# Six staging places at the turn into the down stages, a first tile's norm in eight pieces, and ones-products behind a tile's first chunk

## The chip, the core and the metric

One Trainium2 core runs the whole program. Its engines are TensorE (PE, matmuls, with a separate weight load, PEld), VectorE (DVE), ScalarE (ACT), GpSimd (POOL) and SyncE (SP), which only issues transfers here. Each engine works through its own instructions in order, and semaphores tie them together. The metric is the device time of one execution in microseconds; the median of the runs is compared.

## The reference

The reference is one step of a streaming encoder on 1072 columns (16 meta tokens, 1024 prompt frames, 32 sample frames), with 1024 features:

```python
def rmsnorm(x, g):
    return x * rsqrt(mean(x * x) + EPS) * g

def half_ffn(x, g, w_gate, w_up, w_down):
    h = rmsnorm(x, g)
    return x + 0.5 * ((silu(h @ w_gate) * (h @ w_up)) @ w_down)

x = half_ffn(x, ffn1_norm, ...)
h = rmsnorm(x, mix_norm)
qa, ka, va, zf, ih, qh, g, ga, gb = split(h @ w_in)
oa = stick_breaking_attention(qa, ka, va)      # with the cache for the sample
ob, S = hgrn(qh, sigmoid(zf), ih)              # chunked linear recurrence
x = x + (sigmoid(ga) * (oa @ w_a) + sigmoid(gb) * (norm(ob) * silu(g) @ w_b)) @ w_out
x = half_ffn(x, ffn2_norm, ...)
y = rmsnorm(x, final_norm)
```

The hidden width of both half_ffn is 2816. Outputs are y, the new keys and values, and the final recurrent states.

## The kernel before

**Products.** Every float32 operand is split into a high half (ACT copies it to a rounded type, line 219) and a low half (DVE subtracts, line 220), and each product is made of three matmuls: high by high, high by low, low by high. Line 202 and line 203 do the same for plain weights.

**The two feed-forward blocks** (`Seven`) use seven products of half-size blocks where eight are due. The seven operands made of an activation block are named B11, T3, B21, T2, T4, T1 and B22. The hidden features come in eleven units of 256. The up stage works through the units one after the other, the gate half and then the up half, seven product groups in each (`unit`, `rest`). When a unit is done, `send` queues seven stagings for it. A staging makes one operand (for a T a subtraction on DVE, line 343), splits it into a staging place on chip and lets POOL start the write to `mid_dram` (line 353). `tick`, called after each product group, lets one staging of the unit before go at every odd group. Normal units alternate between two places, called R and st. The last unit's seven stagings, made at the turn into the down stage, take their places from a list (line 325); a place taken a second time must wait until its first write has landed.

**The down stage** (`down`) reads these operands back: `load` and `load_rest` fetch a unit's seven operands into its homes, among them the small tiles xe0, xe1, xe2, xe3 and st in the first block, and mh and st in the second. Its weights come through `lanes` (raw loads, line 528, and sums into S, lines 542 to 545). Its first four jobs use one unit and half of the columns (`singles`), with 84 matmuls; the first and the last stagings are sent around them (`sends(4)`, `sends(3)`). Then come jobs with two units at once, and six singles at the end. A job has seven products p1 to p7: after p1 ACT copies the sum to a second bank (line 600), and the results go out on ACT (line 594) or are added by DVE (line 591). Activation columns are 268 wide per quarter in the first block and 264 in the second.

**Behind the first down stage** comes the next norm, in three column tiles of 400, 384 and 288. `normalise` makes the scaled high and low halves (xh on ACT, xl on DVE, lines 234 and 235), squares them on ACT and adds the squares up, five on POOL into `ms` and three on DVE into `ys` (lines 240 to 244). `finish` multiplies both sums by a matrix of ones on PE and makes R, the scale of the columns, from it. `after1(0)` does the first tile in one go while the last three jobs of down run, and the first `finish` is called after `down`. `project_all` then makes the zf projection: for each tile, three chunks, one for each of three weights, 24 matmuls each, with the rest of the `finish` calls between them.

**What sets the order.** A tile framework gives each engine its list. Instructions are placed by the order of the program and by a priority; PE, while `PE.on` is set, keeps exactly the order in which the code issues (`InOrder`). The buffers of a tag rotate, and a reuse waits until the last reader of the buffer is done.

## Time and profile before

| | us |
|---|---|
| median of three runs | 2502.78 |
| lowest and highest | 2499.66, 2502.88 |
| profiled execution | 2499.49 |
| its span, first to last instruction | 2497.4 |
| PE busy in it | 2403.0 (96%) |
| DVE busy | 1669.2 (67%) |
| ACT busy | 1021.3 (41%) |
| mean granted PE clock | 0.990 |

The profiled execution lies 2.1 us above its own span and 3.3 us under the median. PE is the engine that is busy nearly throughout, and the up stages run without a gap on it. A stretch in which PE stands still or runs at a lower clock is therefore where time can be won or lost. An idle engine that is not PE costs nothing by itself. In a timeline row the bracket at the end gives the idle time of the engine before the instruction and what ended it. A windows row gives the stretch, its length, then busy time and count of PE, PEld, DVE, ACT and POOL, the granted PE clock as a share, the busy share of the transfer engines and GB/s.

### The profile page before, as it was taken

What the parts mean: (1) busy time and instruction counts of PE and PEld (TensorE: products, weight loads), DVE (VectorE), ACT (ScalarE), POOL (GpSimd) and SP (SyncE); (2) the same over time, 40 slices, a digit from 0 to 9 for tenths busy, and PEclk for the clock granted to TensorE, in tenths of its full rate; (3) what the DMA queues carried; (4) which work ended last, traced back from release to release, by engine and by line L of the source; (5) the groups of instructions that cost most, each with busy time, mean ns of one, the idle gap of its engine ahead of it and who ended that gap; (6) DMA issues with size and microseconds to landing.
All of it is one profiled execution on the core that took longest, in us unless ns stands there. A gap on an engine that the chain in (4) does not pass through costs nothing.

```text
span 2497.4 us, 47900 instructions
## 1 busy us (share of the span) xinstructions
PE 2403.0 (96%) x19500; PEld 2299.1 (92%) x19500; DVE 1669.2 (67%) x3144; ACT 1021.3 (41%) x2129; POOL 257.2 (10%) x461
## 2 busy tenths in 40 slices
PE   6999999989998999999999999999799999989997
PEld 5999999979998999999788888999799999989997
DVE  4767676758865377774666665556966767666876
ACT  6444444542225243332545544323544444443223
POOL 1001010100003011221000000111011111110000
PEclk9999999999999999999999999999899999999999
DMA  7334343477651211111211122522244444467761
GB/s 197 105 122 166 122 166 122 164 292 280 245 210 62 60 44 56 48 49 53 57 44 49 44 64 67 190 86 98 75 136 153 143 147 147 143 266 267 274 235 71
DMA packets 270371, 331.93 MB, mean 133 GB/s; under 512 B 41078, under 2 KB 228726, under 8 KB 264518
## 3 DMA queue, kind: packets, MB, share of 16 engines
q1 hardware_dynamic: 247942, 244.96, 29.7%
q0 software_dynamic: 22208, 83.91, 8.9%
q8 instruction: 153, 2.51, 0.4%
q14 instruction: 68, 0.56, 0.1%
HBM read 213.93 MB, written 114.89 MB: 132 GB/s over the span
## 4 chain that ended last, share of the span: by engine, by line
PE 54%; issue 29%; DVE 6%; DMA 4%; POOL 4%; ACT 3%; POOLq 0%; SPq 0%; DVEq 0%; ACTq 0%
PE ps_mm L103 20%; PE ps_z L103 11%; PE pu L103 6%; PE ps_o L103 5%; PE pv L103 4%; PE pf L103 4%; POOL mid_dram L353 3%; DMA mid_dram<-st 2%; PE ps_tr L103 2%; PE ps_tr L106 2%; PE ps_z L106 1%; DMA u_xl<-mid_dram 1%; DVE wlo L203 1%; PE ps_mm L106 0%; DVE acc L1661 0%
## 5 line engine op out<-in xcount | busy, mean ns | idle before, releaser
L103 PE MATMUL ps_mm<-xh,whi 128*128 128x384 f32 (+2 forms) x952 | 316.8, 333 | 0.5 <-DVE raw L1455 0.5
L103 PE MATMUL ps_mm<-xh,wlo 128*128 128x384 f32 (+2 forms) x952 | 310.4, 326 | 0.0
L103 PE MATMUL ps_mm<-xl,whi 128*128 128x384 f32 (+2 forms) x952 | 309.9, 326 | 0.0
L219 ACT ACTIVATE whi<-S 128x1024 fp32r<-128x1024 f32 x122 | 129.2, 1059 | 310.7 <-PE ps_z L103 138.0
L353 POOL DMA_DIRECT2D mid_dram<-st x148 | 102.7, 702 | 872.7 <-DVE st L220 854.9
L103 PEld LDWEIGHTS ps_mm<-xh,whi 128*128 128x128 f32 x952 | 179.3, 188 | 9.0 <-issue 5.0
L103 PEld LDWEIGHTS ps_mm<-xl,whi 128*128 128x128 f32 x952 | 179.4, 188 | 1.1
L103 PEld LDWEIGHTS ps_mm<-xh,wlo 128*128 128x128 f32 x952 | 179.5, 189 | 0.3
L220 DVE TENSOR_TENSOR wlo<-S,whi 128x1024 fp32r<-128x1024 f32 x122 | 149.2, 1223 | 37.8 <-ACT whi L219 35.2
L220 DVE TENSOR_TENSOR st<-g,st 128x536 fp32r<-128x536 f32 (+1 forms) x148 | 103.5, 709 | 100.2 <-ACT st L219 100.1
L1247 DVE TENSOR_TENSOR_SCAN left<-left,oneb 128x512 f32<-128x512 f32 (+6 forms) x112 | 107.4, 959 | 54.8 <-ACT left L119 54.2
L202 ACT ACTIVATE whi<-raw 128x1024 fp32r<-128x1024 f32 x67 | 70.5, 1056 | 172.6 <-PE ps_mm L103 135.8
L219 ACT ACTIVATE st<-g 128x536 fp32r<-128x536 f32 (+1 forms) x148 | 93.5, 643 | 96.6 <-DMA mid_dram<-st 82.4
L220 DVE TENSOR_TENSOR wlo<-raw,whi 128x1024 fp32r<-128x1024 f32 x80 | 76.6, 958 | 72.6 <-ACT whi L219 70.9
L103 PE MATMUL ps_z<-acc1s,whi 128*128 128x268 f32 (+1 forms) x480 | 106.3, 285 | 0.0
L103 PE MATMUL ps_z<-xh1s,whi 128*128 128x268 f32 (+1 forms) x360 | 102.8, 286 | 0.0
L103 PE MATMUL ps_z<-xl1s,whi 128*128 128x268 f32 (+1 forms) x360 | 102.6, 285 | 0.0
L103 PE MATMUL ps_z<-xh1s,wlo 128*128 128x268 f32 (+1 forms) x360 | 102.6, 285 | 0.0
L103 PE MATMUL ps_z<-xh2s,whi 128*128 128x268 f32 (+1 forms) x352 | 100.5, 286 | 2.2 <-ACT s L458 2.2
L103 PE MATMUL ps_z<-xl2s,whi 128*128 128x268 f32 (+1 forms) x352 | 100.4, 285 | 0.0
L103 PE MATMUL ps_z<-xh2s,wlo 128*128 128x268 f32 (+1 forms) x352 | 100.3, 285 | 0.0
L203 DVE TENSOR_TENSOR wlo<-raw,whi 128x1024 fp32r<-128x1024 f32 x67 | 82.8, 1240 | 23.3 <-ACT whi L202 23.1
(719 smaller groups left out, 7636.2 us busy)
## 6 DMA issues: line engine op xcount, KB each, us to landing
mid_dram<-st POOLq DMA_DIRECT2D x74, 536.0 KB, 4.2
mid_dram<-st POOLq DMA_DIRECT2D x74, 528.0 KB, 3.9
raw<-in_ffn_w_gate_dram SPq DMA_DIRECT2D x44, 512.0 KB, 3.8
raw<-in_ffn_w_up_dram SPq DMA_DIRECT2D x44, 512.0 KB, 3.9
raw<-in_w_in_dram SPq DMA_DIRECT2D x44, 512.0 KB, 3.7
raw<-in_ffn_w_down_dram SPq DMA_DIRECT2D x40, 512.0 KB, 5.3
u_xl<-mid_dram SPq DMA_DIRECT2D x8, 1608.0 KB, 6.5
u_xh<-mid_dram SPq DMA_DIRECT2D x8, 1608.0 KB, 10.4
```

Of the source, the lines that this page charges most:

```text
L103: return self.queue(nc.tensor.matmul(*args, **more))
L106: return self.queue(nc.tensor.transpose(*args, **more))
L202: A.activation(hi, raw, AF.Copy)
L203: V.tensor_tensor(lo, raw, hi.bitcast(F32), op=ALU.subtract)
L219: A.activation(dst_h, src, AF.Copy)
L220: V.tensor_tensor(dst_l, src, dst_h.bitcast(F32), op=ALU.subtract)
L353: nc.gpsimd.dma_start(self.mids[i, :, :, NAMES.index(name)], st.bitcast(F32))
L1247: V.tensor_tensor_scan(rev(st[:rows]), rev(st[:rows]), one, 1.0 if carry is None else carry[:rows], op0=ALU.mult, op1=ALU.mult)
```

## The change

It has five parts. The last unit's stagings take six places in place of four, two of them new: the early tiles `e`, which are the first two of the three homes of unit 2 (xe0 and xe1 in the first block, two of mh in the second). Stagings of the other units go out at even instead of odd product groups, and in the gate half of the last unit at every group. The last single job at the turn and the last of the pair jobs are marked "end", which swaps the order of their last products. The norm of the first 400 columns becomes eight works, one for each feature block, that are taken from the queue at every second product of the last jobs (20 // 8 = 2); its POOL sum is kept in R. The tiles of 384 and 288 columns first make all their scaled halves and then all their squares, with DVE's sum in a tile of its own. Last, each `finish` is called behind a tile's first zf chunk.

```diff
@@ -227,29 +227,45 @@
         tag, bufs = homes.get(tag, (tag, bufs))
         return pool.tile([P, width[0]], F32, tag=tag, name=f"t_{tag}", bufs=bufs)
 
-    def normalise(pool, srcs, xh, xl, j, R, t0, n):
+    def normalise(pool, srcs, xh, xl, j, R, t0, n, together=True):
+
         s = slice(t0, t0 + n)
-        for k in range(KC):
+        tots = {}
+
+        def gain(k):
             g = gains[:, j, k:k + 1]
-            A.activation(xh[:, k, s], srcs[k], AF.Copy, scale=g)
+            made = A.activation(xh[:, k, s], srcs[k], AF.Copy, scale=g)
+            if together:
+                tc.add_manual_dep(made.ins, mark[0].name, order, reason="order")
             V.scalar_tensor_tensor(xl[:, k, s], srcs[k], g, xh[:, k, s].bitcast(F32),
                                    op0=ALU.mult, op1=ALU.subtract)
-        tots = []
-        for first, last, eng in ((0, 5, G), (5, KC, V)):
-            tot = temp(pool, "ys" if tots else "ms", 1)
-            A.activation(tot[:, :n], srcs[first], AF.Square)
-            for k in range(first + 1, last):
+
+        def square(k):
+            first = k < 5
+            if first not in tots:
+                tots[first] = R[:, s] if first else (
+                    temp(pool, "ys", 1) if together else
+                    pool.tile([P, width[0]], F32, tag="g", name="tot", bufs=4))[:, :n]
+                A.activation(tots[first], srcs[k], AF.Square)
+            else:
                 sq = temp(pool, "sq")
                 A.activation(sq[:, :n], srcs[k], AF.Square)
-                eng.tensor_tensor(tot[:, :n], tot[:, :n], sq[:, :n], op=ALU.add)
-            tots.append(tot)
+                (G if first else V).tensor_tensor(tots[first], tots[first], sq[:, :n], op=ALU.add)
+            if len(tots) == 2 and k == 7:
+                waiting.append(finish)
 
         def finish():
             ps = bank(rotate=True)
-            PE.matmul(ps[:, :n], ones, tots[0][:, :n], start=True, stop=False)
-            PE.matmul(ps[:, :n], ones, tots[1][:, :n], start=False, stop=True)
+            PE.matmul(ps[:, :n], ones, tots[True], start=True, stop=False)
+            PE.matmul(ps[:, :n], ones, tots[False], start=False, stop=True)
             scale_rows(pool, ps, R, t0, n)
-        waiting.append(finish)
+
+        def both(k):
+            gain(k)
+            square(k)
+        if together:
+            return [lambda k=k: both(k) for k in (0, 5, 1, 2, 6, 3, 4, 7)]
+        return [lambda k=k: gain(k) for k in range(KC)] + [lambda k=k: square(k) for k in (0, 5, 1, 2, 6, 3, 4, 7)]
 
     waiting = []
 
@@ -322,7 +338,7 @@
             self.mids, self.homes = mids, homes
             self.B, self.X, self.ahead = {}, {}, {}
             self.gs, self.later, self.groups = [], [], 0
-            self.stages = ["R", "st", "s", "s", "R", "st", "s"]
+            self.stages = ["R", "e", "e", "st", "s", "s", "R"]
 
         def tile(self, name, shape, dt=F32):
             tag, bufs = self.tags[name]
@@ -347,6 +363,8 @@
                         st = base.tile(shape, F32R, tag="R", name="st")
                     elif at == "st":
                         st = self.pool.tile(shape, F32R, tag="st", name="st", bufs=1)
+                    elif at == "e":
+                        st = self.early.pop(0)
                     else:
                         st = self.tile(at, shape, F32R)
                     split(st[:, :, 0], st[:, :, 1], v)
@@ -361,9 +379,9 @@
             away("T2", b22, b22, b11)
             away("T4", b21, b21, b22)
 
-        def tick(self):
+        def tick(self, every=2):
             self.groups += 1
-            if self.later and self.groups % 2:
+            if self.later and self.groups % every == 0:
                 self.later.pop(0)()
 
         def block(self, w, c):
@@ -478,7 +496,7 @@
                 for step in steps:
                     for b in range(2):
                         step(b)
-                    self.tick()
+                    self.tick(1 if i == FC // 2 - 1 else 2)
 
         def rest(self):
             for i in range(1, FC // 2):
@@ -626,12 +644,12 @@
 
             def run(jobs):
 
-                queue, count = [], [0]
+                queue, count, every = [], [0], [1]
 
                 def step(product):
                     product()
                     count[0] += 1
-                    if queue and count[0] % 5 == 0:
+                    if queue and count[0] % every[0] == 0:
                         queue.pop(0)()
                 before = None
                 for job in jobs:
@@ -644,6 +662,7 @@
                         step(before.p7)
                         if before.done:
                             queue += before.done()
+                            every[0] = max(1, 20 // len(queue))
                     step(job.p3 if job.done == "end" else job.p4)
                     if job.done == "end":
                         step(job.p6)
@@ -669,6 +688,8 @@
             PE.on = True
             W = self.lanes(w, ((0, 2), (0, 3)))
             units.update({i: self.Home(self, i) for i in range(2)})
+            self.early = [self.pool.tile([P, 2, 2, qw], F32R, tag=tag, name="st", bufs=bufs)
+                          for tag, bufs in self.homes[2][:2]]
             for i in range(2):
                 units[i].load_rest()
                 units[i].load(0)
@@ -676,7 +697,9 @@
             for i in range(2):
                 units[i].load(1)
             ahead = self.lanes(w, ((0, 0), (1, 0)), ("raw2", None))
-            run([Job([(units[0], W, l)], 2 + l, b) for b in range(2) for l in range(2)])
+            jobs = [Job([(units[0], W, l)], 2 + l, b) for b in range(2) for l in range(2)]
+            jobs[-1].done = "end"
+            run(jobs)
             sends(3)
             adds = {2: (0,), 3: (4,), 4: (1, 2), 5: (5, 6), 6: (3,), 7: (7,)}
 
@@ -691,7 +714,10 @@
                         if mp % 2:
                             for m in adds.get(s, ()):
                                 add_residual(m)
-                        yield Job([(units[s - 1], W, 0), (units[s], W, 1)], mp)
+                        job = Job([(units[s - 1], W, 0), (units[s], W, 1)], mp)
+                        if s == last and mp == 2:
+                            job.done = "end"
+                        yield job
 
             psum("pairs")
             run(steps())
@@ -871,14 +897,18 @@
             if "R" not in fed:
                 fed.update(xh=big("xh", F32R), xl=big("xl", F32R), R=base.tile([P, T], F32, tag="R", name="R"))
             flat = [a.rearrange("p q n -> p (q n)") for a in ff.acc]
-            for t0, n in TT[1:] if b else TT[:1]:
+            works = []
+
+            def keep(t0, n):
                 for m in range(KC):
                     nc.sync.dma_start(x1_dram[:, m, t0:t0 + n], flat[m][:, t0:t0 + n])
-                normalise(pool, [a[:, t0:t0 + n] for a in flat], fed["xh"], fed["xl"], 1, fed["R"], t0, n)
-            return []
+            for t0, n in TT[1:] if b else TT[:1]:
+                keep(t0, n)
+                works += normalise(pool, [a[:, t0:t0 + n] for a in flat], fed["xh"], fed["xl"], 1, fed["R"], t0, n,
+                                   not b)
+            return works
 
         ff.down(ffn1_w_down, x0_dram, "natural_log_exp_and_others", after1, early1)
-        waiting.pop(0)()
         xh1, xl1, R1 = fed["xh"], fed["xl"], fed["R"]
         homes.clear()
 
@@ -898,11 +928,11 @@
                                      for k in range(KC)])
                     if pending:
                         pending.pop()()
+                    if between and wh is ws[0][0]:
+                        between()
                     later = evac(ps, t0, n)
                     if later:
                         pending.append(later)
-                    if between:
-                        between()
             if pending:
                 pending.pop()()
 
@@ -922,7 +952,7 @@
             return COL_ZF + h * P, evac
 
         PE.on = True
-        project_all([zf_unit(h) for h in range(3)], TT, True, lambda: waiting and waiting.pop(0)(),
+        project_all([zf_unit(h) for h in range(3)], TT, True, lambda: waiting.pop(0)(),
                     [fed["w"]])
         PE.on, PE.last = False, None
```

How the instructions stand on the engines, of before and of the change, at three places:

ACT at the first turn, before. `whi<-S` is the split of weights, `st<-g` and `s<-g` are staging splits of hidden features, `ps_z<-ps_z` is the copy of a job's first sum, `acc1s` are evictions.

```order
L219 ACTIVATE whi<-S 128x1024
L219 ACTIVATE st<-g 128x2x268
L600 ACTIVATE ps_z<-ps_z 128x268
L594 ACTIVATE acc1s<-ps_o 128x268
L594 ACTIVATE acc1s<-ps_z 128x268
L219 ACTIVATE s<-g 128x2x268
L219 ACTIVATE st<-g 128x2x268
L594 ACTIVATE acc1s<-ps_z 128x268
```

The same place of the change (line 600 is now 618, 594 is 612):

```order
L219 ACTIVATE whi<-S 128x1024
L219 ACTIVATE s<-g 128x2x268
L618 ACTIVATE ps_z<-ps_z 128x268
L612 ACTIVATE acc1s<-ps_o 128x268
L612 ACTIVATE acc1s<-ps_z 128x268
L219 ACTIVATE st<-g 128x2x268 x2
L612 ACTIVATE acc1s<-ps_z 128x268
```

The staging split ahead of the first copy is another one, which goes into a tile that no earlier staging has used.

DVE at the end of the first down stage, before. `xl_8300` and `xl_8301` are the low halves of the tiles of 384 and 288 columns, `wlo<-raw,whi` is the low half of a zf weight; the second zf weight's is the first of the two here.

```order
L591 SCALAR_TENSOR_TENSOR acc0s<-ps_o,acc0s 128x268
L203 TENSOR_TENSOR wlo<-raw,whi 128x1024
L591 SCALAR_TENSOR_TENSOR acc0s<-ps_z,acc0s 128x268
...
L235 SCALAR_TENSOR_TENSOR xl_8300<-acc2s,gains,xh_8297 128x384 x2
L235 SCALAR_TENSOR_TENSOR xl_8301<-acc2s,gains,xh_8298 128x288
L235 SCALAR_TENSOR_TENSOR xl_8301<-acc0s,gains,xh_8298 128x288
L244 TENSOR_TENSOR t_ys<-t_ys,t_S 128x384
L235 SCALAR_TENSOR_TENSOR xl_8301<-acc1s,gains,xh_8298 128x288
L244 TENSOR_TENSOR t_ys<-t_ys,t_S 128x384
L203 TENSOR_TENSOR wlo<-raw,whi 128x1024
```

The same place of the change, from the last eviction of the down stage on (line 609):

```order
L609 SCALAR_TENSOR_TENSOR acc0s<-ps_z,acc0s 128x268
L240 SCALAR_TENSOR_TENSOR xl_8300<-acc0s,gains,xh_8297 128x384 x2
L240 SCALAR_TENSOR_TENSOR xl_8300<-acc1s,gains,xh_8297 128x384 x3
L240 SCALAR_TENSOR_TENSOR xl_8300<-acc2s,gains,xh_8297 128x384 x2
L253 TENSOR_TENSOR tot<-tot,t_S 128x384
L240 SCALAR_TENSOR_TENSOR xl_8301<-acc0s,gains,xh_8298 128x288
L240 SCALAR_TENSOR_TENSOR xl_8301<-acc1s,gains,xh_8298 128x288 x2
L240 SCALAR_TENSOR_TENSOR xl_8301<-acc2s,gains,xh_8298 128x288
L253 TENSOR_TENSOR tot<-tot,t_S 128x384
L240 SCALAR_TENSOR_TENSOR xl_8301<-acc2s,gains,xh_8298 128x288
L203 TENSOR_TENSOR wlo<-raw,whi 128x1024
```

The low half of the second zf weight has moved from among the evictions to behind the low halves of both later tiles.

PE in the last jobs of the first down stage, before (`cst` holds the ones):

```order
L103 MATMUL ps_z<-u_xl_7791,raw_8093 128x268
L103 MATMUL ps_tr<-t_ms,cst 128x400
L103 MATMUL ps_z<-u_xh_7559,whi 128x268 x2
...
L103 MATMUL ps_z<-u_xl_7791,raw_8093 128x268
L103 MATMUL ps_tr<-t_ys,cst 128x400
L103 MATMUL ps_z<-u_xe_7561,whi 128x268 x2
```

And the change, where they now stand:

```order
L103 MATMUL ps_tr<-xl_8299,whi 128x400
L103 MATMUL ps_tr<-xh_8296,wlo 128x400
L103 MATMUL ps_z<-R,cst 128x400
L103 MATMUL ps_z<-t_ys,cst 128x400
L103 MATMUL ps_o<-xh_8296,whi 128x400
```

The two ones-products of the first tile have left the products of the down stage and stand between the first zf chunk and the second.

## Rows read from the trace of the kernel before

**Rows 1.** Windows, core 0 (span, busy by engine, PEclk, DMA share, GB/s): turns, steady.

```profile
518.38:545.68 27.30, 16.46 (x86) 14.18 (x84) 14.10 (x26) 12.32 (x30) 4.17 (x6) 0.81 0.94 362
2231.75:2257.61 25.86, 16.07 (x86) 14.27 (x84) 14.13 (x26) 12.28 (x30) 4.17 (x6) 0.80 0.88 347
580.00:620.00 40.00, 40.00 (x326) 40.00 (x325) 34.24 (x62) 10.79 (x20) 0.00 (x0) 1.00 0.78 278
```

**Rows 2.** Timeline of PE, first turn: start, us, operation, [idle before <-releaser].

```profile
524.12 1.04 PE L103 MATMUL ps_z<-u_xh,g 128*128 128x268 f32 x3 [4.84 <-ACT ps_z L600]
...
528.54 0.52 PE L103 MATMUL ps_o<-u_xh,whi 128*128 128x268 f32 x2 [0.82 <-DVE acc1s L591]
...
536.62 0.65 PE L103 MATMUL ps_o<-u_xh,g 128*128 128x268 f32 x3 [3.31 <-ACT acc1s L594]
...
538.42 0.82 PE L103 MATMUL ps_z<-u_xh,whi 128*128 128x268 f32 x2 [0.72 <-ACT acc1s L594]
...
544.56 0.52 PE L103 MATMUL ps_z<-u_xe,whi 128*128 128x268 f32 x2 [0.53 <-DVE acc2s L591]
...
545.68 0.52 PE L103 MATMUL pv<-u_xh,raw 128*128 128x268 f32 x2 [0.48 <-ACT acc2s L594]
```

**Rows 3.** Timeline of ACT, first turn, the two staging splits that wait longest.

```profile
523.14 0.65 ACT L219 ACTIVATE st<-g 128x536 fp32r<-128x536 f32 x1 [5.04 <-DMA mid_dram<-st]
...
535.64 0.65 ACT L219 ACTIVATE st<-g 128x536 fp32r<-128x536 f32 x1 [3.69 <-DMA mid_dram<-st]
```

**Rows 4.** Tile view of mid_dram, 488 to 545 us: waiters and landing times.

```profile
  ACT st L219: 8.7, 2
...
DMA to landing us min/median/max: 3.4/8.2/14.0
```

**Rows 5.** Second turn: rows of ACT's and PE's timeline, and ACT's waits.

```profile
2236.99 0.64 ACT L219 ACTIVATE st<-g 128x528 fp32r<-128x528 f32 x1 [5.50 <-DMA mid_dram<-st]
...
2237.97 1.03 PE L103 MATMUL ps_z<-u_xh,g 128*128 128x264 f32 x3 [5.33 <-ACT ps_z L600]
...
ACT st L219 <- DMA mid_dram<-st: 7.2, 2, 5.5
```

**Rows 6.** Timeline of SP and of DVE around the end of the first turn.

```profile
542.47 1.31 SPq L528 DMA_DIRECT2D raw<-in_ffn_w_down_dram  x2
...
547.71 0.43 DVE L542 TENSOR_TENSOR S<-raw 128x256 f32<-128x256 f32 x1 [3.20 <-DMA raw<-in_ffn_w_down_dram]
```

**Rows 7.** Windows: the full queues of turn one, then two behind down.

```profile
519.00:541.00 22.00, 12.17 (x67) 10.56 (x66) 11.91 (x23) 10.74 (x26) 3.63 (x6) 0.84 0.97 388
...
762.40:767.00 4.60, 4.60 (x18) 3.75 (x19) 2.49 (x6) 1.02 (x2) 0.00 (x0) 0.63 0.21 75
...
781.40:786.00 4.60, 1.77 (x6) 0.86 (x6) 3.95 (x7) 3.47 (x8) 2.44 (x3) 1.00 0.00 0
```

**Rows 8.** Timeline of PE at the end of the first down stage.

```profile
762.37 1.39 PE L103 MATMUL ps_tr<-t_ms,cst 128*128 128x400 f32 x2 [3.90 <-POOL t_ms L244]
...
776.89 0.34 PE L103 MATMUL ps_z<-xh,whi 128*128 128x400 f32 x1
...
781.08 0.35 PE L103 MATMUL ps_z<-xh,wlo 128*128 128x400 f32 x1
```

**Rows 9.** Timeline of DVE and of POOL in the same stretch.

```profile
778.68 1.66 DVE L235 SCALAR_TENSOR_TENSOR xl<-acc1s,gains,xh 128x384 fp32r<-128x384 f32 x3
...
780.26 3.06 DVE L235 SCALAR_TENSOR_TENSOR xl<-acc2s,gains,xh 128x384 fp32r<-128x384 f32 x3
...
785.76 1.23 DVE L203 TENSOR_TENSOR wlo<-raw,whi 128x1024 fp32r<-128x1024 f32 x1 [0.65 <-ACT whi L202]
...
780.33 2.67 POOL L244 TENSOR_TENSOR t_ms<-t_ms,t_S 128x384 f32<-128x384 f32 x2 [4.18 <-ACT t_S L243]
```

**Rows 10.** Page part 5: costliest groups, the staging splits on ACT and DVE.

```profile
L219 ACT ACTIVATE st<-g 128x536 fp32r<-128x536 f32 (+1 forms) x148 | 93.5, 643 | 96.6 <-DMA mid_dram<-st 82.4
...
L220 DVE TENSOR_TENSOR st<-g,st 128x536 fp32r<-128x536 f32 (+1 forms) x148 | 103.5, 709 | 100.2 <-ACT st L219 100.1
```

## The prediction

> **What bounds the kernel now.** I read the page first: TensorE (PE) is busy over almost the whole span, so time can only be won where PE stands still or runs at a low clock. The windows show where. In a steady down stretch 326 matmuls take 40.00 us at granted clock 1.00, 0.1227 us each. The two turns from up to down hold 84 matmuls each, worth 84 x 0.1227 = 10.3 us, and last 27.30 and 25.86 us [rows 1]. Next I read PE's own timeline there: six stops, 4.84, 0.82, 3.31, 0.72, 0.53 and 0.48 us, 10.70 in all, and the two long ones end with an ACT instruction, the copy of line 600 and the eviction of line 594 [rows 2]. ACT's timeline says why: directly ahead of both stand staging splits of line 219 that sat 5.04 and 3.69 us until an earlier staging write had landed [rows 3]. The tile view agrees: 8.7 us in two waits, with landings of 3.4 to 14.0 us [rows 4]. ACT is in order, so PE's evictions queue behind a DMA. The second turn repeats it: ACT waits 5.50 us, PE 5.33, and 7.2 us in two ACT waits [rows 5]. The rest of the loss is the clock: 0.81 and 0.80 over the turns [rows 1], so PE's 84 matmuls are busy 16.46 and 16.07 us instead of 10.3. It falls after the first stop, so it should come back with the stop.
>
> **Part 1, the staging places.** Before, the last up unit's seven stagings take the places R, st, s, s, R, st, s: the second user of R waits for the first one's write, and so does the second user of st. After, they take R, two early tiles, st, s, s, R: only the last staging waits, for the write that was issued first. The work is unchanged: seven splits on ACT and on DVE, seven writes on POOL, which has nothing else to do there. The two ACT waits (5.04 + 3.69) go [rows 3]. What is late next? DVE has 14.10 us of work in the first turn and ACT 12.32; PE has 10.3 at full clock [rows 1]. So DVE is the floor of the stage. To it I add the last two stops, 0.53 + 0.48, in which PE waits for the last evictions [rows 2]: 15.1 us. The ends: 10.3 + the four short stops 2.55 = 12.9, if part of DVE's work slides out of the stage, and 27.30 - 4.84 - 3.31 = 19.2, if only the stops go and the clock stays low. I take 15.1, since the floor is a sum of rows: 27.30 - 15.1 = 12.2 gained. In turn two DVE's 14.13 + 1.0 = 15.1: 25.86 - 15.1 = 10.8 gained. Its ends, in the same way: 12.9 us at best (13.0 gained), and at worst only ACT's two waits go, 25.86 - 7.2 = 18.7 (7.2 gained) [rows 1, 5].
>
> Something comes back. The first loads of unit 2 into the early tiles must now wait for two staging writes to land, and SP is in order: the loads of the st place, the next raw weights of down and the residuals queue behind. DVE already waited 3.20 us for those weights, issued 542.47, used 547.71, without a stop of PE [rows 6]. With PE 12 us sooner part of that turns into a PE stop: 0 to 3.20, I take half, 1.6, in each turn: 3.2 lost.
>
> **Part 2, staging of earlier units moved by one product group.** No instruction more or less; the writes on POOL move along. The page has ACT idle for 82.4 us before staging splits, on landings [rows 10], yet PE is not stopped in the up stage, where its neighbours have slack. The move puts the last staging of each unit at its very end. It costs nothing where the pair split 643 + 709 ns [rows 10] hides beside the next products, and at most 1.35 us in each of nine units of both FFNs, 24.3 us, if nothing hides it. I take 0.5 in all: the spacing of two product groups between stagings is unchanged. The two jobs now marked "end" swap the order of their last products and add none: 0.
>
> **Part 3, the first tile's norm and the ones-products.** Removed: PE's stop of 3.90 us for the POOL sum inside the singles of down [rows 8], the slow stretch after it (4.60 us at clock 0.63, 4.60 x 0.37 = 1.7 lost) and 4.60 - 1.77 = 2.83 us of idle at the second tile's ones-products [rows 7]: 8.4 in all. Added is a wait the diff does not show. In the order, DVE's low half of the second zf weight (line 203) now stands behind the low halves of the second and third tile and two sums. After the last eviction DVE has ahead of it seven instructions of 384 columns, 1.66 / 3 = 0.55 each, five of 288, some 0.43 as an estimate scaled by columns (0.55 x 288/384 = 0.41), two sums of some 0.55, and its own 1.23 [rows 9]: 3.9 + 2.1 + 1.1 + 1.2 = 8.3 us. PE meanwhile has the first zf chunk's last 19 products and two ones-products, 21 x 0.182 (24 products from 776.89 to 781.08: 4.19 us over 23 steps) = 3.8 [rows 8]. PE stops for 8.3 - 3.8 = 4.5 us, and the sum would be -3.9. But where POOL's sums ran (780.33, 2.67 us) three of the same DVE instructions took 3.06 instead of 1.66 us [rows 9]: 1.02 each. At that price seven cost 7.1, the stop is 7.7, and the sum is -0.7. POOL still makes five of each tile's eight sums, and the sums ahead of the weight wait for squares from ACT, which now come behind all sixteen gains. I take -1, near the second end. SP issues the weights after those later too, behind the stores of x1, under some 70 zf products of 0.182 us, 13 us: 0. If the stop also drags the clock, as after 762.37, 1.7 come back, and a second weight, 1.23 + 0.65 us later [rows 9], adds 1.9: +2.9.
>
> The Trainium skill (SBUF — State Buffer, section Who interferes with whom) says that a DVE instruction with two SBUF inputs and a GpSimd instruction that reads SBUF lock each other out; the 1.02 against 0.55 us agrees. By that rule alone every low half beside a POOL sum takes the longer price, and part 3 gives 0.7 instead of 3.9.
>
> **The sum.** -12.2 - 10.8 + 3.2 + 0.5 - 1.0 = -20.3. Against the profiled execution's own 2499.49 us that is 2479.2; the median of the runs is 2502.78, 3.3 above it, so the median should be **2482.5**.
>
> **The rivals.** (a) The forecast: 2482.5, by itself 2476 to 2488. (b) **The turns become DMA-bound.** In 519 to 541 us the queues are 0.97 busy at 388 GB/s [rows 7]. The turn moves 362 GB/s x 27.30 us = 9.88 MB, at 388 GB/s 25.5 us; the second 347 x 25.86 = 8.97 MB, 23.1 us [rows 1]. If all of it had to land in the stage, only 1.8 + 2.7 = 4.5 would be won, -5.0 with parts 2 and 3 (the raw wait then lies in the bound). Against: PE was stopped by ACT alone, never by a load, the single products need only unit 0, and the pair stage keeps 0.78 of the queues busy [rows 1], so the rest can spill. Halfway between -20.3 and -5.0: 2490. By the Trainium skill (DMA: Bandwidth & Descriptors, section Issuing engines are not separate DMA queues) writes started on GpSimd interleave with SP's loads on the same 16 engines, so staged writes pulled forward delay the loads; no row here separates the two. (c) **The zf weight's stop** is larger than the stops removed: +2.9 for -1.0, 2486.4. (d) **Part 3 is clean** (-3.9) and the raw weights cost nothing: 2476.4. (e) **Slower: the moved stagings.** The pair split lands in front of the next unit's first evictions and PE waits for it in 18 units: +24.3 for +0.5 gives +3.5, 2506. It decides from 20.8 / 18 = 1.16 us in each unit. Against: PE is stopped by no staging now, and ACT and DVE have slack there. (f) **The places do not come free** (the early tiles still hold operands of the last up products, or ACT waits as before on R): both turns keep their waits, 2501 to 2503. Against: the last up product ends as the first staging is due, and six of seven have a place of their own.
>
> **Chances.** (a) 0.57, (b) 0.14, (c) 0.09, (d) 0.08, (e) 0.06, (f) 0.06. 0.2% is 5.0 us, about what a measurement of this kernel can tell from no change. Faster by more than that, (a) to (d): 0.87 (0.01 of (b), fully bound, goes to the next); within it: 0.07; slower 0.06. The range: up to 2494 it holds most of (b) and (c), down to 2474 all of (d) with PE's lower end of the turns; left out are (e), (f) and the rest of (b), some 0.2.
>
> **What would show it.** Right: ACT's waits of line 219 on mid_dram at the turns fall from 8.7 and 7.2 us to under 2; the turns last 14 to 17 us at a clock near 1.00; the pairs' first weights show a PE stop of 1 to 2 us; no PE stop at the ones-products, but one of 4 to 8 us for the second zf weight's low half; PE stays without stops in the up stages. Wrong: PE waiting for a load in the singles (b), an ACT wait still there (f), stops at each up unit's start (e), or a clock that stays at 0.8 without stops.

## Result and the profile after

| | before | changed |
|---|---|---|
| median, us | 2502.83 | 2479.65 |
| lowest to highest | 2499.66 to 2505.11 | 2478.34 to 2480.68 |
| profiled execution | 2499.49 | 2480.68 |
| its span | 2497.4 | 2478.8 |
| mean granted PE clock | 0.990 | 0.991 |

The ratio is 0.9909, with a 95% interval of 0.9897 to 0.9921: 23 us faster, where 20.3 were forecast (2482.5, range 2474 to 2494). The span of the profiled execution is 18.6 us shorter. What is read from single traces below can account for these 18.6 us; the 23 stand in the medians.

The windows of the two turns come first, cut as in [rows 1], from the first product of the down stage to the first pair job:

```profile
514.07:529.83 15.76, 12.41 (x86) 10.76 (x84) 13.65 (x26) 11.74 (x30) 4.19 (x6) 1.00 1.01 415
...
2223.47:2240.05 16.58, 13.35 (x87) 11.91 (x85) 13.62 (x26) 11.69 (x30) 4.18 (x6) 0.90 1.01 410
```

27.30 us have become 15.76 and 25.86 have become 16.58. The granted clock of the first turn is back at 1.00; in the second it is 0.90. DVE has nearly as much to do as before (13.65 us for 14.10, in a turn of 15.76). The busy share of the transfer engines now stands at 1.01 over both turns, at 415 and 410 GB/s. PE's timeline of the first turn, to be held against [rows 2]:

```profile
517.56 0.52 PE L103 MATMUL ps_z<-u_xh,whi 128*128 128x268 f32 x2 [0.73 <-ACT acc1s L612]
...
519.09 0.52 PE L103 MATMUL ps_o<-u_xh,whi 128*128 128x268 f32 x2 [0.90 <-DVE acc1s L609]
...
526.00 0.51 PE L103 MATMUL ps_z<-u_xh,whi 128*128 128x268 f32 x2 [0.43 <-ACT ps_z L618]
...
528.72 0.52 PE L103 MATMUL ps_z<-u_xe,whi 128*128 128x268 f32 x2 [0.58 <-DVE acc2s L609]
...
529.83 0.64 PE L103 MATMUL pv<-u_xh,raw 128*128 128x268 f32 x3 [0.48 <-ACT acc2s L612]
```

The stops of 4.84 and 3.31 us are gone. What is left in this turn are stops of 0.43 to 0.90 us, 3.12 in all, each ended by an ordinary eviction or copy. The second turn keeps one longer stop, for an eviction on DVE:

```profile
2229.00 0.81 PE L103 MATMUL ps_o<-u_xh,whi 128*128 128x264 f32 x2 [2.41 <-DVE acc1s L609]
```

ACT has no wait on a staging write left in either turn, against [rows 3, 5].

Behind the first turn the work that no longer fits into it shows. These are 20 us of the pair jobs, before:

```profile
545.68:565.68 20.00, 20.00 (x162) 20.00 (x162) 10.91 (x22) 9.86 (x18) 0.00 (x0) 1.00 0.37 135
```

and after the change:

```profile
529.83:549.83 20.00, 19.11 (x151) 18.89 (x152) 7.97 (x18) 8.78 (x17) 0.00 (x0) 1.00 0.81 303
```

The rate is 303 GB/s where it was 135, so (303 - 135) x 20 us = 3.4 MB moved into the pair jobs. The turn itself moves 415 x 15.76 = 6.5 MB where it moved 9.9. SP, ACT and PE show the price:

```profile
514.64 0.44 SPq L519 DMA_DIRECT2D u_xl<-mid_dram  x1
...
530.51 1.92 SPq L528 DMA_DIRECT2D u_xe<-mid_dram  x2
...
533.40 0.52 SPq L528 DMA_DIRECT2D u_st<-mid_dram  x1
...
533.97 1.16 SPq L546 DMA_DIRECT2D raw<-in_ffn_w_down_dram  x2
...
542.91 0.64 PE L103 MATMUL pv<-u_xh,g 128*128 128x268 f32 x3 [0.88 <-ACT pu L618]
...
541.33 1.03 ACT L219 ACTIVATE g<-raw 128x256 fp32r<-128x256 f32 x3 [4.53 <-DMA raw<-in_ffn_w_down_dram]
```

Unit 2's loads into the early tiles (`u_xe`) start at 530.51, 15 us behind the load in front of them, and `u_st` and the raw weights follow. ACT sits 4.53 us on the weights (541.33), and PE stops for 0.88 us behind it. [rows 6] showed such a wait in the kernel before without any stop of PE: there the weights were issued 3.2 us before the first pair job began (542.47 for 545.68), here 4.1 us behind its start (533.97 for 529.83).

Last comes the end of the down stage, which answers to [rows 7 to 9]: ACT, DVE and PE around the second zf weight, and the window behind the stop:

```profile
754.75 1.05 ACT L202 ACTIVATE whi<-raw 128x1024 fp32r<-128x1024 f32 x1
...
770.68 1.21 DVE L203 TENSOR_TENSOR wlo<-raw,whi 128x1024 fp32r<-128x1024 f32 x1
...
772.79 2.06 DVE L203 TENSOR_TENSOR wlo<-raw,whi 128x1024 fp32r<-128x1024 f32 x1
...
771.95 0.70 PE L103 MATMUL ps_o<-xh,wlo 128*128 128x400 f32 x1 [6.85 <-DVE wlo L203]
...
771.95:777.00 5.05, 5.05 (x15) 5.00 (x16) 3.88 (x3) 0.78 (x2) 4.95 (x5) 0.50 0.52 144
```

The stops of 3.90, 1.63 and 1.20 us for the sums have gone. Two stops of 0.53 and 0.52 us for evictions on DVE have come among the last jobs, and one of 6.85 us for the low half of the second zf weight. ACT had its high half ready at 755.8; DVE, in order, came to it at 770.68. For 5.05 us after the stop the clock stands at 0.50.

### The profile page after: what moved, and what is told of

Its sections match the earlier page's. It is cut to its first block, busy times and chain, and to the rows that moved or that the text cites. A ratio compares the mean times of both kernels' runs of the same rounds, so it can differ in the third digit from the quotient of the medians.

```text
span 2478.8 us, 47913 instructions
## 1 busy us (share of the span) xinstructions
PE 2401.1 (97%) x19500; PEld 2297.4 (93%) x19500; DVE 1670.0 (67%) x3144; ACT 1017.5 (41%) x2129; POOL 257.3 (10%) x461
## 4 chain that ended last, share of the span: by engine, by line
PE 82%; DVE 7%; issue 4%; DMA 4%; ACT 2%; POOL 1%; SPq 0%; DVEq 0%; ACTq 0%; POOLq 0%
PE ps_mm L103 27%; PE ps_z L103 25%; PE ps_o L103 9%; PE pu L103 6%; PE ps_tr L103 5%; PE pf L103 4%; PE pv L103 4%; PE ps_tr L106 2%; DMA mid_dram<-st 2%; DMA raw<-in_ffn_w_down_dram 1%; PE ps_z L106 1%; DMA u_xl<-mid_dram 1%; DVE wlo L203 1%; POOL mid_dram L371 1%; DVE xl L240 0%
```

## Experiments

All ratios are against the kernel before, run on the same chip.

**The places alone.** The six places and the denser staging of the last unit's gate half, on the kernel before:

```diff
-            self.stages = ["R", "st", "s", "s", "R", "st", "s"]
+            self.stages = ["R", "e", "e", "st", "s", "s", "R"]
...
+                    elif at == "e":
+                        st = self.early.pop(0)
...
-                    self.tick()
+                    self.tick(i == FC // 2 - 1)
...
```

> The kernel before with the six staging places alone: the list R, two early tiles, st, s, s, R, and, in the gate half of the last unit, a staging at every product group; nothing of the norm, the ones-products, the even groups or the end marks. If the staging wait is the cause of the gain, both turns shorten as in the change (27.30 to about 15.8 us, 25.86 to about 16.5) and some 3 us come back in the pair jobs: 20.9 - 3 = 18 us faster, about 2485. If a good part of the 23 us came from the other parts (the up stage began its turn 4.3 us earlier in the changed kernel's trace, from parts not in this kernel), it gains more or less than that: 12 us or less if the turn's gain needs the other parts.

Measured: 2485.08 us, ratio 0.993 (0.9912 to 0.9948), 18 us faster. Its two turns:

```profile
514.58:530.66 16.08, 12.67 (x87) 10.80 (x85) 13.73 (x26) 11.75 (x30) 4.18 (x6) 1.00 1.01 409
...
2224.83:2241.15 16.32, 12.57 (x86) 10.69 (x85) 13.60 (x26) 11.56 (x30) 4.18 (x6) 1.00 1.01 411
```

They last 16.08 and 16.32 us, as in the change. The turns need nothing of the other parts. The time is 5 us above the change's, though the two intervals overlap (0.9912 to 0.9921).

**The change without its places.** The other way round:

```diff
-            self.stages = ["R", "e", "e", "st", "s", "s", "R"]
+            self.stages = ["R", "st", "s", "s", "R", "st", "s"]
...
-            self.early = [self.pool.tile([P, 2, 2, qw], F32R, tag=tag, name="st", bufs=bufs)
-                          for tag, bufs in self.homes[2][:2]]
```

> The change without its six places: the list of the last unit's stagings is R, st, s, s, R, st, s again and no early tiles are taken; norm, ones-products, even groups and end marks stay. If the places carry the gain, both ACT waits on an earlier staging write come back at the turns, which last 25 to 27 us again, and the time is 2498 to 2503. If the earlier and denser staging of the last unit's gate half, or the even groups, already free the places in time, the turns stay under 20 us and the time is under 2490.

Measured: 2497.79 us, ratio 0.9977 (0.9967 to 0.9986). The windows of its turns and ACT's wait in the first:

```profile
513.64:538.29 24.65, 15.96 (x87) 14.21 (x85) 14.08 (x26) 12.41 (x30) 4.15 (x6) 0.79 0.94 380
...
2227.05:2253.46 26.41, 17.20 (x86) 15.63 (x84) 14.13 (x26) 12.36 (x30) 4.15 (x6) 0.74 0.89 351
...
ACT st L219 <- DMA mid_dram<-st: 6.7, 2, 5.1
```

Both turns are back at 24.65 and 26.41 us, at a clock of 0.79 and 0.74, with 6.7 us of ACT's waits on staging writes in the first. The places carry the gain of the turns. This kernel is still 5 us faster than the one before.

**One wait put back.**

```diff
-            self.stages = ["R", "e", "e", "st", "s", "s", "R"]
+            self.stages = ["R", "e", "st", "st", "s", "s", "R"]
...
-                          for tag, bufs in self.homes[2][:2]]
+                          for tag, bufs in self.homes[2][:1]]
```

> The change with one staging wait put back: the list is R, one early tile, st, st, s, s, R, so that the fourth staging must wait until the third one's write has landed; everything else as in the change. If ACT's waits on landings are what the turns lost, this one wait costs what such a wait cost before, 4 to 5 us on ACT, 3 to 5 us of a PE stop, and 1 to 3 us of slow clock behind it, in each turn: +8 to +14 us, 2488 to 2494. If the turns are now bound by the transfer engines (busy share 1.01 over the whole of both turns in the change's trace), the wait hides beside them: within 2 us of the change.

Measured: 2491.49 us, ratio 0.996 (0.9945 to 0.9975), 12 us slower than the change. The waiting split on ACT, PE behind it, and the window of the first turn:

```profile
530.53 0.65 ACT L219 ACTIVATE st<-g 128x536 fp32r<-128x536 f32 x1 [6.53 <-DMA mid_dram<-st]
...
531.51 0.81 PE L103 MATMUL ps_z<-u_xh,whi 128*128 128x268 f32 x2 [7.06 <-ACT acc1s L612]
...
512.70:537.62 24.92, 15.08 (x87) 13.61 (x85) 13.86 (x26) 12.11 (x30) 4.16 (x6) 0.79 0.94 376
```

One ACT wait of 6.53 us makes one PE stop of 7.06, the mean clock of the turn falls to 0.79, and the turn lasts 24.92 us. A single landing in ACT's order costs here what two did in the run above: this one wait is as long as those two together (6.7 us), and the clock falls with either.

**The staging writes made twice.** This asks whether the transfer engines bound the turns:

```diff
                     nc.gpsimd.dma_start(self.mids[i, :, :, NAMES.index(name)], st.bitcast(F32))
+                    if i == FC // 2 - 1:
+                        twice = dram.tile(shape, F32, tag=f"twice{self.qw}{name}", name="twice")
+                        nc.gpsimd.dma_start(twice, st.bitcast(F32))
```

> The change, with each of the last unit's seven staging writes made a second time, into a scratch tensor that nobody reads: 7 x 0.536 = 3.75 MB more to move at each turn, no compute more. If the turns go by DVE's and ACT's work (13.65 us of DVE in 15.76) and the loads have slack, the turns stay under 18 us and the time within 4 us of the change, up to 2484. If the turns or the pair jobs' loads behind them are bound by the transfers, each turn with what follows pays 3.75 MB / 411 GB/s = 9.1 us: 2498.

Measured: 2498.68 us, ratio 0.999 (0.9981 to 1.0): 19 us slower than the change, close to the 2 x 9.1 that the bytes alone would give. The first turn and the 20 us behind it, SP's issue of the next weights, ACT's wait for them, and PE's stop:

```profile
512.94:530.13 17.19, 12.81 (x86) 10.81 (x85) 13.73 (x26) 11.82 (x30) 5.65 (x9) 1.00 1.01 414
...
530.13:550.13 20.00, 12.17 (x96) 11.95 (x96) 1.17 (x3) 2.91 (x6) 1.78 (x3) 0.86 1.04 406
...
539.10 2.54 SPq L549 DMA_DIRECT2D raw<-in_ffn_w_down_dram  x2
...
ACT g L219 <- DMA raw<-in_ffn_w_down_dram: 12.6, 1, 12.6
...
551.27 1.04 PE L103 MATMUL pv<-u_xh,g 128*128 128x268 f32 x3 [8.97 <-ACT pu L621]
```

The turn itself grows from 15.76 to 17.19 us only, and first turns of kernels with single writes last 15.4 to 17.2 us too (the odd groups back, the norm of before). The rest is paid in the pair jobs: ACT waits 12.6 us for raw weights and PE 8.97 us behind it. So the loads did have slack within the turn, but none in the turn and the first pair jobs together. The weights came late in two ways: SP issued them 5.1 us later than in the change (539.10 for 533.97), since the loads ahead of them had to wait for the doubled writes, and they took some 3 us longer to land.

**The same, with those weights first.** Is it the place of the weights in SP's order, or the bytes? Unit 2's last loads are put behind the weights of the third pair job; those of the fourth stay where they were:

```diff
+                        if s == 1 and mp == 0:
+                            early_raw = {(1, 1): self.fetch(w, ((0, 1), (1, 1))), (2, 2): self.fetch(w, ((1, 2), (2, 2)))}
                         if mp % 2 == 0 and s < last:
-                            units[s + 1] = self.home(s + 1)
+                            units[s + 1] = self.home(s + 1, self.fetched if s == 1 else None)
...
```

> The sixth experiment (each staging write of the turn made twice, 19 us slower than the change) with one difference: the raw down weights of the third pair job are issued on SP ahead of unit 2's loads, so that they no longer stand behind the loads that wait for the doubled staging writes. If the 19 us came from the place of these weights in SP's order (ACT waited 12.6 us for them, PE 9.0 us), most of it goes: 2480 to 2487. If they came from the bytes, with the transfer engines full, the weights land as late as before or something else does: 2494 or more.

Measured: 2503.68 us, ratio 1.0001 (0.9991 to 1.001), not better. SP's two issues, DVE's waits for them, and PE at the place of the stop:

```profile
508.86 0.41 SPq L549 DMA_DIRECT2D raw<-in_ffn_w_down_dram  x1
...
541.51 0.57 SPq L549 DMA_DIRECT2D raw<-in_ffn_w_down_dram  x1
...
530.32 0.43 DVE L568 TENSOR_TENSOR S<-raw 128x256 f32<-128x256 f32 x1 [1.89 <-DMA raw<-in_ffn_w_down_dram]
...
551.51 0.43 DVE L568 TENSOR_TENSOR S<-raw 128x256 f32<-128x256 f32 x1 [8.91 <-DMA raw<-in_ffn_w_down_dram]
...
553.29 0.81 PE L103 MATMUL pu<-u_xe,whi 128*128 128x268 f32 x2 [5.57 <-DVE acc0s L617]
```

PE's stop of 8.97 us is gone, and one of 5.57 us stands one product later: DVE sits 8.91 us on the fourth job's weights, and the eviction that PE waits for stands behind them. The third job's weights, issued at 508.86, were still waited for at 530, 21 us later, so an early issue did not bring them early. That speaks for the bytes. It does not settle it: the fourth job's weights still stand behind unit 2's loads on SP (541.51), which wait for the doubled writes, and no run here has the bytes without that wait.

**Zf weights early.** The second and third zf weight are made ahead of the later tiles' norms (`late` makes the next weight; it is called behind the fourth of the last six jobs and behind the last):

```diff
+            if late:
+                jobs[3].done = late
             run(jobs)
+            if late:
+                late()
             for work in after(1):
...
-                    [fed["w"]])
+                    fed["w"])
...
```

> The change, with the second zf weight made as soon as the fourth of the last six jobs has issued its products and the third right behind the last job, both ahead of the later tiles' norms, so that their low halves no longer stand behind sixteen scaled halves on DVE. If DVE's order alone makes the 6.85 us stop of PE, the stop and the half-clock stretch behind it go (6.85 + 2.5): 2470 to 2472. If something else is due right behind (the scale R, the third weight, ACT's squares), a stop of 3 to 6 us stands at another product and the time is 2476 to 2480.

Measured: 2471.77 us, ratio 0.9877 (0.9863 to 0.9892), 8 us faster than the change and the fastest kernel here. The two low halves on DVE, PE's two stops in that stretch, and the window that answers to the slow one of the change:

```profile
748.83 1.21 DVE L203 TENSOR_TENSOR wlo<-raw,whi 128x1024 fp32r<-128x1024 f32 x1
...
759.79 1.21 DVE L203 TENSOR_TENSOR wlo<-raw,whi 128x1024 fp32r<-128x1024 f32 x1
...
759.99 0.45 PE L103 MATMUL ps_tr<-xh,whi 128*128 128x400 f32 x1 [0.80 <-ACT xh L237]
...
761.60 0.45 PE L103 MATMUL ps_tr<-xl,whi 128*128 128x400 f32 x1 [1.16 <-DVE xl L240]
...
771.00:777.00 6.00, 6.00 (x36) 6.00 (x35) 1.47 (x4) 1.01 (x3) 5.30 (x6) 1.00 0.00 0
```

The low halves now stand at 748.83 and 759.79. Of the 6.85 us, stops of 0.80 and 1.16 us are left, and the clock is 1.00 behind them. DVE's order made the stop: ACT's high half was ready 15 us before DVE came to the low one.

**Weights first, on this kernel.** With both edits together:

> The fourth experiment (zf weights early, 2471.8) with the raw down weights of the third pair job ahead of unit 2's loads. In the change's trace ACT waits 4.5 us for them and PE 0.88 us behind it, and the pair jobs gave back 1.7 us at the first turn. If that is their place in SP's order, 1 to 3 us are won over both blocks: 2469 to 2471. If PE's stop there has another cause, 2471 to 2472.

Measured: 2477.48 us, ratio 0.9893 (0.9878 to 0.9908), about 4 us slower than with the zf weights alone, though the intervals overlap by 0.0014. The stop behind the pair weights went, and others came in the turns. DVE and PE in the first, and the windows of both:

```profile
527.81 0.43 DVE L565 TENSOR_TENSOR S<-raw 128x256 f32<-128x256 f32 x1 [2.25 <-DMA raw<-in_ffn_w_down_dram]
...
528.97 0.51 PE L103 MATMUL ps_z<-u_xe,whi 128*128 128x268 f32 x2 [2.32 <-DVE acc2s L614]
...
512.59:530.09 17.50, 12.39 (x86) 10.77 (x85) 15.13 (x31) 12.78 (x33) 4.20 (x6) 1.00 1.02 406
2214.38:2234.67 20.29, 15.22 (x86) 13.58 (x85) 15.50 (x32) 12.87 (x33) 4.20 (x6) 0.83 1.00 406
```

DVE, in order, now waits 2.25 us for the weights within the turn, and PE 2.32 us for DVE's eviction, where it was 0.58 in the change. The work on these weights now lies in the turn as well (15.13 us of DVE for 13.65), and the turn lasts 17.50 us. The second turn, at 20.29 us and a clock of 0.83, loses more; with the zf weights alone the two last 15.77 and 15.68 us. The price of the late loads was moved here, not removed.

**The norm of before.** The change with the old norm, all at once, and the old place of the ones-products:

```diff
-        if together:
-            return [lambda k=k: both(k) for k in (0, 5, 1, 2, 6, 3, 4, 7)]
...
+        for k in range(KC):
+            g = gains[:, j, k:k + 1]
...
-                    if between and wh is ws[0][0]:
-                        between()
...
+                    if between:
+                        between()
...
```

> The change with the norm behind the first down stage and its ones-products as in the kernel before; places, groups and end marks stay. Forecast of the prediction: the norm's part gains 1 us, so this kernel is 1 us slower than the change, 2481. The traces of the change say otherwise: from the end of the pair jobs to the second zf tile it lost some 4 us (a stop of 6.85 us and a slow clock behind it for stops of 3.90, 1.63 and 1.20 us), so this kernel should be faster, about 2475.

Measured: 2479.27 us, ratio 0.9909 (0.9893 to 0.9926), the time of the change. The norm's part is worth nothing that can be told either way; the two intervals leave room for some 5 us. My expectation of 2475, read from two single traces, fell: in this kernel too the last down jobs and the zf chunks took longer than in the profiled execution of the kernel before. Counted by PE's starts, that is from the start of the 5500th matmul in a trace to that of the 5900th, the norm of before takes 69.0 us in the kernel before and 73.1 here (72.2 with the places alone, which has the same norm), and the new norm 73.3 in the change.

**Groups, end marks, the dense last unit.** There are four small edits; this is the first:

```diff
-            if self.later and self.groups % every == 0:
+            if self.later and (every == 1 or self.groups % 2):
```

> The change with the stagings of all but the last unit at odd product groups again. Forecast of the prediction: the move costs 0.5 us at most, so 2479 to 2480. The traces show a PE stop of 2.17 us in the first staged unit of the kernel before (1.2 us with the odd groups in the first experiment) and of 1.0 or less with the even groups: if that is the groups' doing, this kernel is 1 to 4 us slower than the change, 2481 to 2484.

Measured: 2479.63 us, 0.991 (0.9896 to 0.9925).

> The change without both end marks (the last single job at the turn, the last pair job). The prediction took them as 0: 2479.6. The traces say that the mark on the last pair job ended two stops of PE at the step from pairs to singles (0.81 and 1.08 us, 2.1 us gained in all) in each block, and nothing is known of the other: 2482 to 2484.

Without both end marks: 2478.19 us, 0.9909 (0.9894 to 0.9924). The stops that the mark on the last pair job ended (0.84 and 1.00 us here) are paid in the change a few products later, at the first singles (0.61 and 0.69 us).

> The kernel before with one difference: in the gate half of the last unit a staging goes out at every product group. The second experiment (the change without its six places) was 5 us faster than the kernel before, though undoing the norm, the even groups and the end marks singly each cost the change nothing that can be told. If the denser staging made these 5 us (its first turn took 24.65 us against 27.30), it is 2497 to 2500; if not, 2502 to 2503.

Measured: 2502.78 us, 0.9992 (0.9983 to 1.0001).

> The kernel before with one difference: all stagings that tick lets go stand at even product groups. The prediction priced the move at 0 to 0.5 us of loss. The traces with odd groups show one PE stop of 2.17, 1.2 and 2.3 us in the first staged unit (the kernel before, the first and the seventh experiment), twice with a half-clock stretch behind it, those with even groups 1.0 us or less. If that is the groups' doing, this kernel is 2 to 4 us faster than the kernel before, 2498 to 2501, and makes most of the 5 us by which the change without its places was faster; if not, 2502 to 2504.

Measured: 2500.05 us, 0.9991 (0.9983 to 1.0). None of the four differs from what it is compared with by more than its interval. The trace shows one thing that the prediction had denied, a PE stop in the up stage behind a staging. These are ACT's and PE's timelines in the first staged unit of the kernel before, where the copy that PE waits for stands behind a staging split that waits for a landing:

```profile
115.13 0.65 ACT L219 ACTIVATE st<-g 128x536 fp32r<-128x536 f32 x1 [2.98 <-DMA mid_dram<-st]
...
116.11 0.39 PE L103 MATMUL ps_z<-xh2s,whi 128*128 128x268 f32 x1 [2.17 <-ACT s L458]
```

PE's of the change with the odd groups back, with the window behind it:

```profile
114.13 0.39 PE L103 MATMUL ps_z<-xh2s,whi 128*128 128x268 f32 x1 [2.29 <-ACT s L476]
...
115.00:124.00 9.00, 9.00 (x64) 9.00 (x63) 7.38 (x10) 4.91 (x11) 0.52 (x1) 0.83 0.38 119
```

and of the change itself:

```profile
111.88 0.39 PE L103 MATMUL ps_mm<-xh0s,whi 128*128 128x268 f32 x1 [1.00 <-ACT s L476]
```

With odd groups it is 2.17 and 2.29 us, with a mean clock of 0.79 and 0.83 over the 8 and 9 us behind it, but only 1.2 and 1.4 us in the traces of the places alone and of the dense last unit, which keep a clock of 1.00. With even groups it is 1.00 us or less in all ten traces.

## Why the prediction was right, point by point

**The cause.** ACT's order behind staging writes was the loss at the turns, and the places took it away. The places alone, the change without them and the one wait put back say so from three sides, and the denser staging without the places gains nothing that can be told (0.9992). The forecast of the first turn, 15.1 us by DVE's work and two last stops, met 15.76; the second met 16.58 for 15.1, with one PE stop of 2.41 us behind a DVE eviction in it and a clock of 0.90. Gained in the traces: 11.5 and 9.3 us for 12.2 and 10.8. The clock came back with the stops, fully in the first turn. That DVE's work is what now sets the turn's length is argued from its busy share (13.65 of 15.76 us). The weights-first kernel, with 15.13 us of DVE work in 17.50, agrees with it, but DVE also waits 2.25 us for a load there. One reading was loose: the 3.4 to 14.0 us of [rows 4] are landings of all transfers on mid_dram, SP's loads included. The staging writes alone took 3.4 to 10.3 us there, and 8.6 to 12.9 in the change's first turn, where nothing on ACT waits for them any more.

**What comes back.** The loads of unit 2 do wait for staging writes and hold up SP, and the weights come late (ACT 4.53 us, PE 0.88). The term was 1.6 us for each turn. By PE's starts, matmul by matmul, the first pair jobs gave back 1.7 us behind the first turn and 0.6 behind the second, 2.3 for the 3.2 forecast. In the five other traces with the places and single writes, those with the weights moved on SP left out, both turns together gave back 2.2 to 4.5 us. The term had the right size and the right mechanism.

**Rival (b), the transfers.** It did not decide this change, but it was nearer than its chance of 0.14 says. My argument against it, that the rest can spill into the pair jobs, held: 3.4 MB did. (That PE was stopped "by ACT alone" was not exact: two of the six stops in [rows 2], 0.82 and 0.53 us, ended with DVE.) But 3.75 MB more at each turn cost the time of all their bytes. Had I set the 9.9 MB of the first turn against what the turn and the next 20 us can carry together, some 35.8 us x 0.41 MB/us = 14.7 MB, I would have seen a room of 2.1 MB: before, they carried 9.9 + 135 x 20 / 1000 = 12.6. Even this sum is too kind. By it the doubled writes exceed the room by 1.65 MB, 4.0 us at each turn, and the runs cost 9 to 10. Which loads wait for which writes counts beside the bytes, and the runs do not part the two.

**The norm's part.** Forecast -1, measured 0, with room for some 5 us either way. The stop for the second zf weight was worked out as 4.5 to 7.7 us and is 6.85. The fall of the clock behind it, which I kept for rival (c), came too: 5.05 us at 0.50 cost 2.5. The second weight's own stop of rival (c) did not: DVE was through with it (772.79 + 2.06) before PE came to it. By these rows the part is -8.4 + 6.85 + 2.5 = +0.9. The -8.4 was read from a good execution of the kernel before: by PE's starts the old norm's stretch took 69.0 us in that trace and in one other, and 72.2 to 73.1 in three more. It also left out the new stops for evictions (0.53 and 0.52 us).

**The moved stagings.** "PE is stopped by no staging now" was wrong in the first staged unit of the first block (2.17 us). The even groups shorten that stop instead of adding one, so rival (e) fell by its sign. In the time this is some 2 us, with an interval of 0 to 4 (0.9991, 0.9983 to 1.0, alone).

**The size.** 20.3 forecast, 23.2 by the medians, 18.6 by the two profiled executions. Before the turn the changed kernel's trace is already 4.3 us ahead (514.07 for 518.38). The 2.17 us stop and its slow clock are part of that. At the 100th matmul, ahead of any staging, the changed kernel leads by 1.9 us, at the 700th by 4.1; in the traces of the places alone, the dense last unit and the odd groups back, all three with odd groups, the lead at the 700th is 3.6, 4.1 and 2.0 us. So most of it belongs to the profiled execution of the kernel before rather than to the change. By PE's starts the two turns with their pair jobs gained 18.5 us, where 12.2 + 10.8 - 3.2 = 19.8 were forecast, and 3.8 were lost from the end of the pair jobs through the norm. The places alone made 18 us in the medians. So the main term was right in mechanism and size. The other 5 us, for which the forecast had 0.5, have no known cause, and that 23 lies so near 20.3 with them in it is in part luck.

**What stays open.** The change without its places is still 5 us faster than the kernel before (0.9977, 0.9967 to 0.9986). The dense last unit and the even groups alone give ratios of 0.9992 and 0.9991, which together would make 4 of the 5, but each lies at the edge of its interval. Undone singly with the places in, the norm, the groups and the end marks cost nothing. Which of them makes these 5 us, or whether they add up only together, isn't settled.

## What to carry to other kernels

Where an in-order engine both prepares buffers for a write and empties PE's banks, a buffer reused before its write has landed stops PE: give the burst as many places as it has buffers, borrowed from tiles that are loaded later, and look which load then waits for them. Price such a step by the next floor (here DVE's 14.1 us and the bytes of the stage), not by the stop alone, and add the clock that goes with a stop. After a reordering, look for operands that only stand late in another engine's order: making the two zf weights earlier was worth 8 us more here, without any work removed.

## What the runs showed of the hardware

- The granted clock makes a stop dearer than it is: a PE stop of 6.85 us was followed by 5.05 us at 0.50, a turn with a stop of 7.06 us had a mean of 0.79, and in the fastest kernel stops of 0.80 and 1.16 us left it at 1.00.
- The transfer engines ran for 15.76 us at a busy share of 1.01 and 415 GB/s without a stop of PE on any of the turn's loads; 7.5 MB more over two turns cost 19 us. With the engines this full, staging writes of 0.536 MB took 8.6 to 12.9 us to land; over the whole kernel the median is 4.1.
- POOL held DVE up again: in the change DVE's low halves of 384 columns took 0.94 us each where POOL added beside them, 0.55 us where it did not. The Trainium skill (SBUF — State Buffer, section Who interferes with whom) says that a DVE instruction with two SBUF inputs contends with a GpSimd instruction that reads SBUF, and this trace agrees:

```profile
762.33 1.66 DVE L240 SCALAR_TENSOR_TENSOR xl<-acc1s,gains,xh 128x384 fp32r<-128x384 f32 x3
...
763.92 1.88 DVE L240 SCALAR_TENSOR_TENSOR xl<-acc2s,gains,xh 128x384 fp32r<-128x384 f32 x2
...
763.64 1.20 POOL L253 TENSOR_TENSOR R<-R,t_S 128x384 f32<-128x384 f32 x1 [3.84 <-ACT t_S L252]
```
